# Seven quadrant products in place of eight in twelve gate/up blocks of an FFN, with the weight sums made by accumulating transfers

## The chip, the core and the metric

One core of one Trainium2 chip runs the whole kernel. The metric is the device time of one launch in microseconds. The kernel before took 1153.77 us (median of 3 runs, 1153.56 to 1154.09).

TensorE (PE) multiplies, VectorE (DVE) and ScalarE (ACT) work element by element, GpSimd (POOL) does a few small operations, SyncE (SP) issues the DMA transfers. Each engine works through its own queue in order, and semaphores order the engines among each other.

## The reference

Two layers; each has a first FFN, a mixer (state-space model and chunked attention) and a second FFN. The change is in the two FFNs of each layer.

```python
def rmsnorm(x, g):
    y = xf * lax.rsqrt(jnp.mean(xf * xf, axis=-1, keepdims=True) + RMS_EPS)
    return (y * g.astype(jnp.float32)).astype(x.dtype)

def swiglu(h, w_gate, w_up, w_down):
    return (jax.nn.silu(h @ w_gate) * (h @ w_up)) @ w_down

def reference(x, ...):                    # x: (1, 256, 1024) float32
    for l in range(DEPTH):                # DEPTH = 2
        f1 = swiglu(rmsnorm(x, g[0]), ffn_w_gate[l, 0], ffn_w_up[l, 0], ffn_w_down[l, 0])
        x = x + 0.5 * rmsnorm(f1, g[1])
        m = hybrid_mixer(rmsnorm(x, g[2]), w_in[l], ...)
        x = x + rmsnorm(m, g[3])
        f2 = swiglu(rmsnorm(x, g[4]), ffn_w_gate[l, 1], ffn_w_up[l, 1], ffn_w_down[l, 1])
        x = x + 0.5 * rmsnorm(f2, g[5])
    return x
```

The model width is 1024 and the FFN width 2816.

## The kernel before

The 256 rows of x are two row tiles of 128, t = 0 and t = 1. All weights are packed on the host into 368 chunks of 128 x 1024 float32 (512 KB) in the order of their use. `weight(i)` loads chunk i with one DMA into a `raw` buffer and splits it: ACT copies it to `wh` in a reduced format (fp32r), and DVE writes the rest, `wl = raw - wh`. Activations are split in the same way into `xh` and `xl`. A product of 128 x 128 by 128 x 512 is then three matmuls into one bank of PSUM (`ps`): xh by wh, xh by wl, xl by wh (`mm`, line 400 of the kernel before).

An FFN goes over its width in blocks of 512 (`N_BLK`: five of 512 and one of 256). A block of 512 takes for each row tile a gate product and an up product (`gemm`, four chunks each, six matmuls a chunk and row tile), then the gate's SiLU on ACT, its product with up on DVE, four transposes on PE and the split of their result (`t_split`), and one block later four down chunks (`gemm_wide`: three matmuls for each half of the 1024 columns, so six a chunk and row tile) that add to two `ps` banks for each row tile. So a block has 144 matmuls of 512 columns: 96 for gate and up, 48 for down. The program has 20 blocks of width 512; the change touches 12 of them.

The program is recorded as a graph of operations (`Graph.op`), each with a cost in microseconds, and `schedule` lists them: due times run back from the end (`MARGIN` says how much earlier a stream must be done than its user's due time, `TAU` is the time of six matmuls), and at each step the engine that is free first takes the candidate that is due first. `SLOTS` says how many buffers of a class there are: 4 `raw`, 8 `wh`, 8 `wl`, 28 `blk` of 128 x 512, 8 `ps`. The resulting list sets the order on every engine, and the buffers. The times of the list are plans; on the chip an operation starts when its engine has come to it and its semaphores allow it. A load (`dma`, on SP's queue) waits on DVE's `wl` of the chunk that had its `raw` buffer before. `prep` computes the state-space constants of a layer, mainly in small DVE operations, somewhere in the layer's first FFN. `boundary` ends an FFN or a mixer: norm, residual and the next left-hand sides.

## Time and profile before

| | before |
|---|---|
| runs: median (lowest to highest) | 1153.77 us (1153.56 to 1154.09) |
| span of the profiled execution | 1151.6 us |
| PE busy in the span | 1140.8 us, 99% |
| DVE busy | 788.6 us, 68% |
| ACT busy | 606.3 us, 53% |
| POOL busy | 19.8 us, 2% |
| DMA: moved, mean share of the 16 engines | 205.02 MB, 53.7% on the loads' queue |

The profiled execution is given by its span, from the first to the last instruction; the median of the runs is 2.2 us above it, for what lies outside the first and the last instruction. The rows of the page name engine, line and tiles; a line is mostly that of a helper (`mm` is L400, `act` L358, `tt` L365, the transposes L414), so the tiles tell what is meant: `wh<-raw` is the first half of a conversion, `wl<-raw,wh` the second. "Idle before" tells how long the engine stood just ahead of such an instruction and what ended that. The FFNs take about 8 to 200, 385 to 577, 577 to 770 and 955 to 1145 us of the span, the mixers what is between.

### The profile page before, as it was taken

How to read it: one execution, taken by the hardware profiler on the slowest of the kernel's cores; microseconds unless marked ns; L12 is line 12 of the kernel's file. 1: busy time of each engine (PE TensorE's matmuls, PEld its weight loads, DVE VectorE, ACT ScalarE, POOL GpSimd, SP SyncE). 2: the span in 40 equal slices, each digit the busy share in tenths (PEclk: the TensorE clock that was granted, in tenths of full speed). 3: DMA queues.
4: the chain of work that ended last, by engine and by line, in shares of the span. 5: the costliest groups of instructions: out<-in, count | busy, mean ns of one | idle time of the engine just before them, and what ended most of it. 6: DMA issues, size and time to landing. Idle time of an engine off the chain costs nothing.

```text
span 1151.6 us, 15538 instructions
## 1 busy us (share of the span) xinstructions
PE 1140.8 (99%) x5872; PEld 914.0 (79%) x5872; DVE 788.6 (68%) x1190; ACT 606.3 (53%) x894; POOL 19.8 (2%) x53
## 2 busy tenths in 40 slices
...
GB/s 291 252 195 159 183 219 166 181 164 130 86 189 178 207 200 184 186 182 184 187 220 193 184 150 200 204 177 147 166 110 145 184 198 163 192 192 181 190 165 37
DMA packets 60267, 205.02 MB, mean 178 GB/s; under 512 B 7072, under 2 KB 7840, under 8 KB 60192
## 3 DMA queue, kind: packets, MB, share of 16 engines
q1 hardware_dynamic: 60192, 204.03, 53.7%
...
## 4 chain that ended last, share of the span: by engine, by line
PE 94%; ACT 4%; issue 1%; DMA 0%; SPq 0%; DVE 0%; POOLq 0%; POOL 0%; DVEq 0%
PE ps L400 89%; PE ps L414 4%; ACT utz L358 2%; PE ps L406 1%; ACT blk L358 1%; ACT wh L358 1%; DMA x<-in_x_dram 0%; SPq L341 0%; DVE x L380 0%; POOLq L1139 0%; POOL s L376 0%; DVEq L1139 0%; DVE s L388 0%; POOLq L376 0%
## 5 line engine op out<-in xcount | busy, mean ns | idle before, releaser
L400 PE MATMUL ps<-wh,blk 128*128 128x512 f32 x2944 | 916.4, 400 | 0.0
L400 PEld LDWEIGHTS ps<-wh,blk 128*128 128x128 f32 x2944 | 548.0, 188 | 122.6 <-issue 0.3
L365 DVE TENSOR_TENSOR wl<-raw,wh 128x1024 fp32r<-128x1024 f32 (+1 forms) x370 | 448.7, 1217 | 281.9 <-ACT wh L358 280.6
L358 ACT ACTIVATE wh<-raw 128x1024 fp32r<-128x1024 f32 (+1 forms) x370 | 389.7, 1055 | 374.5 <-PE ps L400 334.1
L400 PE MATMUL ps<-wl,blk 128*128 128x512 f32 x1472 | 551.7, 399 | 0.0
L400 PEld LDWEIGHTS ps<-wl,blk 128*128 128x128 f32 x1472 | 274.8, 188 | 61.1 <-issue 0.3
L358 ACT ACTIVATE blk<-ps 128x512 fp32r<-128x512 f32 (+3 forms) x136 | 78.1, 583 | 121.5 <-PE ps L414 103.3
L365 DVE TENSOR_TENSOR blk<-ps,blk 128x512 fp32r<-128x512 f32 (+2 forms) x104 | 69.0, 666 | 36.1 <-ACT blk L358 34.9
L414 PE MATMUL ps<-ident,blk 128*128 128x128 f32 x432 | 76.8, 273 | 0.2
L414 PEld LDWEIGHTS ps<-ident,blk 128*128 128x128 f32 x432 | 57.0, 140 | 20.1 <-ACT blk L358 1.0
L358 ACT ACTIVATE blk<-ps,s 128x512 f32<-128x512 f32 (+1 forms) x80 | 52.5, 658 | 27.6 <-PE ps L400 25.6
L380 DVE SCALAR_TENSOR_TENSOR blk<-ps,s,blk 128x512 f32<-128x512 f32 (+1 forms) x48 | 33.8, 703 | 15.3 <-PE ps L400 11.5
L376 POOL TENSOR_TENSOR s<-s,mhalf 128x1 f32<-128x1 f32 x24 | 13.8, 574 | 804.0 <-DVE s L388 799.1
L358 ACT ACTIVATE blk<-blk,s 128x128 f32<-128x128 f32 (+1 forms) x64 | 25.8, 444 | 0.0
L400 PEld LDWEIGHTS ps<-utz,bt 128*128 128x128 f32 x128 | 18.1, 191 | 4.0 <-ACT utz L358 2.8
L365 DVE TENSOR_TENSOR blk<-blk,blk 128x512 f32<-128x512 f32 (+3 forms) x38 | 21.1, 577 | 0.1
L358 ACT ACTIVATE utz<-blk 32x128 f32<-32x128 f32 x64 | 20.1, 314 | 1.0
L358 ACT ACTIVATE blk<-blk 64x128 f32<-64x128 f32 (+2 forms) x44 | 17.1, 393 | 6.5 <-DVE blk L380 6.0
L365 DVE TENSOR_TENSOR blk<-blk,e 128x512 f32<-128x512 f32 x32 | 20.3, 677 | 0.0
L400 PE MATMUL ps<-utz,bt 128*128 128x128 f32 x128 | 19.2, 278 | 1.0 <-ACT utz L358 0.8
L365 DVE TENSOR_TENSOR blk<-ps,e 128x512 f32<-128x512 f32 x32 | 19.9, 677 | 0.0
L856 DVE TENSOR_TENSOR_SCAN blk<-mt,blk 128x512 f32<-128x512 f32 x16 | 18.6, 1203 | 0.0
...
## 6 DMA issues: line engine op xcount, KB each, us to landing
raw<-in_wall_dram SPq DMA_DIRECT2D x366, 512.0 KB, 3.5
gain<-in_gains_dram SPq DMA_DIRECT2D x22, 256.0 KB, 4.6
blk<-in_bias_dram SPq DMA_DIRECT2D x8, 256.0 KB, 5.0
raw<-in_wall_dram SPq DMA_DIRECT2D x4, 256.0 KB, 3.5
blk<-in_sp_dram SPq DMA_DIRECT2D x4, 256.0 KB, 4.0
x<-in_x_dram SPq DMA_DIRECT2D x3, 256.0 KB, 5.5
out_dram<-x SPq DMA_DIRECT2D x2, 256.0 KB, 2.0
...
```

What stands on the lines that cost most here:

```text
L358: self.nc.scalar.activation(out=out.ap(), in_=in_.ap(), func=func, **k)
L365: lambda: self.nc.vector.tensor_tensor(out=out.ap(), in0=a.ap(), in1=b.ap(), op=op))
L376: lambda: self.nc.gpsimd.tensor_tensor(out=out.ap(), in0=a.ap(), in1=b.ap(), op=ALU.pow))
L380: return self.g.op("dve", cost, [out], [a, s, b], lambda: self.nc.vector.scalar_tensor_tensor(out=out.ap(), in0=a.ap(), scalar=ap(s), in1= ...
L400: return self.g.op("pe", cost, [out], [lhsT, rhs], lambda: self.nc.tensor.matmul(out.ap(), lhsT=lhsT.ap(), rhs=rhs.ap(), start=start, stop ...
L406: self.nc.tensor.matmul(out.ap(), lhsT=lhsT.ap(), rhs=rhs.ap(), start=start, stop=stop)
L414: lambda o=o, s=s: self.nc.tensor.transpose(o.ap(), s.ap(), self.ident.ap()))
L856: self.g.op("dve", 0.6, [o], [mt, z], lambda o=o, z=z: self.nc.vector.tensor_tensor_scan(out=o.ap(), data0=mt.ap(), data1=z.ap(), initial= ...
```

## The change

In blocks 1 and 3 of each layer's first FFN and blocks 1 to 4 of its second, the gate and up products of both row tiles are taken as one product of 2 by 2 quadrants. The left side has the quadrants a11, a12 (row tile 0, first and second half of the 1024 inputs) and a21, a22 (row tile 1); the right side b11, b21 (gate, two chunks each) and b12, b22 (up). Seven products of sums of quadrants (the Winograd form) give the four results that eight products gave.

- `sums` makes the sums of left quadrants once per FFN: eight DVE additions, four scaled splits (ACT and DVE each) and two negations on ACT.
- `seven` does a block. The weight sums are made in the `raw` buffers: b12, then b21, are negated in place on ACT (four chunks, `raw<-raw`), and `add_to` issues eight accumulating DMAs, 512 KB each, from POOL's queue, with source and destination both in SBUF: b11 += -b12; b12 becomes b22 - b12; b11 += b22; b21 becomes b11 - b21. Between these the contents are converted: 14 conversions for the seven products, where there were 8 for gate and up. The eight `raw` buffers of a block's b quadrants so stay in use for most of the block.
- The products go to the banks p1, p5, p6, p7; ACT copies p1 and DVE reads p5 and p7 in the middle of an accumulation, which then goes on in the same bank. Five DVE additions make the four results from the banks.
- Matmuls of 512 columns in such a block: 84 + 48 in place of 96 + 48. In the whole program 4272 in place of 4416.
- Both row tiles of an FFN are recorded together, block by block (`ffn`).
- `SLOTS`: `raw` 9 for 4, `wh` and `wl` 7 for 8. The planner's costs: a matmul of 512 columns 0.232 for 0.216 us, a scan 1.12 for 0.6; `TAU` 1.395 for 1.355; `MARGIN` of `prep` 40 for 111.6. An accumulating DMA is planned at 0.9 us on POOL and 4.6 us after it.
- `uTz`, two own buffers that were zeroed once, become `blk` buffers that POOL zeroes in each `s5`.

Line numbers grow: `mm` is L416 in the changed kernel, `act` L369, `tt` L376, the transposes L430, `add_to` L380.

```diff
+SEVEN = (((1, 3), (1, 2, 3, 4)), ((1, 3), (1, 2, 3, 4)))
...
-SLOTS = {"blk": 28, "ps": 8, "wh": 8, "wl": 8, "raw": 4, "gain": 2,
+SLOTS = {"blk": 28, "ps": 8, "wh": 7, "wl": 7, "raw": 9, "gain": 2,
          "s1": 16, "s2": 8, "s4": 12, "s16": 8}
-TAU = 1.355
-MARGIN = {"conv": 7.558, "conv0": 3.423, "task": 7.748, "att0": 37.576, "s50": 37.749, "att1": 28.585, "s51": 29.753, "prep": 111.598}
+TAU = 1.395
+MARGIN = {"conv": 7.558, "conv0": 3.423, "task": 7.748, "att0": 37.576, "s50": 37.749, "att1": 28.585, "sums": 8.0, "s51": 29.753, "prep": 40.0}
+ADD_LAT = 4.6
...
+        if a.func == "dma":
+            return ADD_LAT
...
-                b.end = max(b.end, o.end + (DMA_LAT if e == "dma" else HOP))
+                b.end = max(b.end, o.end + (DMA_LAT if e == "dma" else ADD_LAT if o.func == "dma" else HOP))
...
+    def add_to(self, out, in_):
+        return self.g.op("pool", 0.9, [out], [out, in_],
+                         lambda: self.nc.gpsimd.dma_start(out=out.ap(), in_=in_.ap(), accum_op=ALU.add), func="dma")
...
-            cost = n / 2370
+            cost = 0.0049 + n / 2254
...
+    def load(self, i, parts=(slice(0, 1024),)):
+        raw = self.g.buf("raw", [P, 1024])
+        for s in parts:
+            self.last_raw = self.dma(raw[:, s], self.w_d[i][:, s], after=[self.last_raw] if self.last_raw else [])
+        return raw
+
+    def halves(self, raw, parts=(slice(0, 1024),)):
+        wh, wl = self.g.buf("wh", [P, 1024], F32R), self.g.buf("wl", [P, 1024], F32R)
+        for s in parts:
+            self.act(wh[:, s], raw[:, s], AF.Copy)
+            self.tt(wl[:, s], raw[:, s], wh[:, s].bitcast(F32), ALU.subtract)
+        return wh, wl
...
-    def mm_two_k(self, bank, xs, w, first, last):
+    def mm_two_k(self, bank, xs, w, first, last, again=False):
         wh, wl = w
         for i, (xh, _) in enumerate(xs):
             s = slice(i * 512, (i + 1) * 512)
-            self.mm(bank, xh, wh[:, s], first and i == 0, False)
-            self.mm(bank, xh, wl[:, s], False, False)
+            self.mm(bank, xh, wh[:, s], first and i == 0, False, again)
+            self.mm(bank, xh, wl[:, s], False, False, again)
         for i, (_, xl) in enumerate(xs):
-            self.mm(bank, xl, wh[:, i * 512:(i + 1) * 512], False, last and i == len(xs) - 1)
+            self.mm(bank, xl, wh[:, i * 512:(i + 1) * 512], False, last and i == len(xs) - 1, again)
...
+    def wide_step(self, banks, x, w, first):
+        for n in range(2):
+            s = slice(n * 512, (n + 1) * 512)
+            self.mm(banks[n], x[0], w[0][:, s], first, False)
+            self.mm(banks[n], x[0], w[1][:, s], False, False)
+            self.mm(banks[n], x[1], w[0][:, s], False, False)
...
+    def sums(self, xs):
+        self.mode("sums", "bulk")
+        a = []
+        for t in range(2):
+            for hi, lo in xs[t].full:
+                r = self.blk()
+                self.tt(r, hi.bitcast(F32), lo.bitcast(F32), ALU.add)
+                a.append(r)
+        a11, a12, a21, a22 = a
+        self.tt(a22, a21, a22, ALU.add)
+        self.tt(a21, a11, a21, ALU.subtract)
+        self.tt(a11, a22, a11, ALU.subtract)
+        self.tt(a12, a12, a11, ALU.subtract)
+        out = []
+        for r, k in ((a22, -1.0), (a11, 1.0), (a21, 1.0), (a12, 1.0)):
+            hi, lo = self.blk(F32R), self.blk(F32R)
+            self.act(hi, r, AF.Copy, scale=k)
+            self.stt(lo, r, k, hi.bitcast(F32), ALU.mult, ALU.subtract)
+            out.append((hi, lo))
+        hi, lo = self.blk(F32R), self.blk(F32R)
+        for o, v in zip((hi, lo), xs[1].full[1]):
+            self.act(o, v.bitcast(F32), AF.Copy, scale=-1.0)
+        out.append((hi, lo))
+        self.mode()
+        return out
...
+    def seven(self, b, xs, rs, s, acc, pend, first):
+        i = self.chunk[0]
+        assert self.chunk == [i, i]
+        self.chunk = [i + 12, i + 12]
+        t0 = i * 2 * TAU - self.saved
+        self.saved += 2 * TAU
+        for t in range(2):
+            for n in range(12):
+                self.mark[(t, i + n)] = len(self.g.ops)
+
+        def conv(raws):
+            return [self.halves(r) for r in raws]
+
+        self.mode("conv", "main")
+        def minus(raws):
+            for r in raws:
+                self.act(r, r, AF.Copy, scale=-1.0)
+
+        def add(to, raws):
+            for o, r in zip(to, raws):
+                self.add_to(o, r)
+
+        b11 = [self.load(i), self.load(i + 1)]
+        w1 = conv(b11)
+        self.weight(i + 2)
+        b21 = [self.load(i + 3), self.load(i + 4)]
+        w2 = conv(b21)
+        minus(b21)
+        b12 = [self.load(i + 5), self.load(i + 6)]
+        minus(b12)
+        add(b11, b12)
+        w5 = conv(b11)
+        b22 = [self.load(i + 7), self.load(i + 8)]
+        add(b12, b22)
+        add(b11, b22)
+        w6 = conv(b11)
+        self.weight(i + 9)
+        w7 = conv(b12)
+        w3 = conv(b22)
+        self.weight(i + 10)
+        add(b21, b11)
+        w4 = conv(b21)
+        self.weight(i + 11)
+
+        def prod(at, bank, a, w, start):
+            self.mode("main", "main", t0 + at * TAU)
+            pairs = list(zip(self.cols(a[0]), self.cols(a[1])))
+            for u in range(2):
+                self.mm_two_k(bank, pairs[2 * u:2 * u + 2], w[u], start and u == 0, u == 1, not start)
+            self.mode()
+
+        def down(at, c):
+            for t in range(2):
+                self.mode("main", "main", t0 + (at + t) * TAU)
+                self.wide_step(acc[t], pend[t][c], self.weight(i + (2, 9, 10, 11)[c]), first and c == 0)
+            self.mode()
+
+        a11, a12 = xs[0].full
+        s1, s2, s3, s4, a22 = s
+        p1 = self.ps()
+        prod(0, p1, a11, w1, True)
+        k1 = self.blk()
+        self.act(k1, p1, AF.Copy)
+        down(2, 0)
+        prod(4, p1, a12, w2, False)
+        sil = [self.blk(), self.blk()]
+        self.act(sil[0], p1, AF.Silu, scale=rs[0])
+        p5, p6 = self.ps(), self.ps()
+        prod(6, p5, s1, w5, True)
+        prod(8, p6, s2, w6, True)
+        u2, u4 = self.blk(), self.blk()
+        self.tt(u2, p6, k1, ALU.add)
+        self.tt(u4, p5, u2, ALU.add)
+        down(10, 1)
+        p7 = self.ps()
+        prod(12, p7, s3, w7, True)
+        self.tt(u4, p7, u4, ALU.add)
+        prod(14, p5, s4, w3, False)
+        h = [self.blk(), u4]
+        self.tt(h[0], p5, u2, ALU.add)
+        self.stt(h[0], h[0], rs[0], sil[0], ALU.mult, ALU.mult)
+        down(16, 2)
+        prod(18, p7, a22, w4, False)
+        self.tt(u2, p7, u2, ALU.add)
+        self.act(sil[1], u2, AF.Silu, scale=rs[1])
+        self.stt(h[1], h[1], rs[1], sil[1], ALU.mult, ALU.mult)
+        down(20, 3)
+        return [self.t_split(h[t], 4) for t in range(2)]
...
+    def ffn(self, l, f, normed):
         ipost = 1 if f == 0 else 5
         nxt = (l, 2) if f == 0 else (l + 1, 0)
+        xs, rs = (list(z) for z in zip(*normed))
+        acc = [(self.ps(), self.ps()) for _ in range(2)]
+        pend, first, s, pre = None, True, None, [None, None]
         for b, wd in enumerate(N_BLK):
+            if b in SEVEN[l][f]:
+                if s is None:
+                    s = self.sums(xs)
+                pend = self.seven(b, xs, rs, s, acc, pend, first)
+                first = False
+            else:
+                res = []
+                for t in range(2):
+                    sil, h = self.blk(), self.blk()
+                    gb = self.gemm(t, xs[t])
+                    if rs[t] is None:
+                        rs[t] = self.row_scale(t, [self.g.ops[self.mark[(t, 2)]]])
+                    self.act(sil[:, :wd], gb[:, :wd], AF.Silu, scale=rs[t])
+                    up = self.gemm(t, xs[t]) if wd == 512 else gb[:, wd:]
+                    self.stt(h[:, :wd], up, rs[t], sil[:, :wd], ALU.mult, ALU.mult)
+                    res.append(self.t_split(h, wd // P))
+                    if b == len(N_BLK) - 1:
+                        pre[t] = self.pre_gain(t, *nxt)
+                    if pend is not None:
+                        self.gemm_wide(t, acc[t], pend[t], first, False)
+                if pend is not None:
+                    first = False
+                pend = res
             if b == 3:
                 self.gain(l, ipost)
                 if nxt[0] < DEPTH:
                     self.gain(*nxt)
+        out = []
+        for t in range(2):
+            self.gemm_wide(t, acc[t], pend[t], False, True)
+            out.append(self.boundary(t, l, ipost, acc[t], 1.0 / 16, 4.0 * EPS, *nxt, pre[t]))
+        return out
...
-        self.uTz = [self.own(f"utz{i}", [P, 2, 2, 2, 64]) for i in range(2)]
         self.S = [self.own(f"st{i}", [P, PAIRS, 65], F32) for i in range(2)]
-        for t in self.CT + [self.D0] + self.uTz:
+        for t in self.CT + [self.D0]:
...
+        uz = [self.blk() for _ in range(2)]
+        for z in uz:
+            self.memset("pool", z, 0.0)
+        uz = [z.rearrange("p (a b c t) -> p a b c t", a=2, b=2, c=2) for z in uz]
...
-                self.g.op("dve", 0.6, [o], [mt, z], lambda o=o, z=z: self.nc.vector.tensor_tensor_scan(
+                self.g.op("dve", 1.12, [o], [mt, z], lambda o=o, z=z: self.nc.vector.tensor_tensor_scan(
...
-            normed = [self.ffn(t, l, 0, normed[t]) for t in range(2)]
+            normed = self.ffn(l, 0, normed)
...
+        if i in seven:
+            out += [gu[i][:2], dn[i - 1][:1], gu[i][2:], dn[i - 1][1:]]
+        else:
+            out += [gu[i], dn[i - 1]]
```

Three places show the order on the engines. In the names `raw`, `wh`, `wl`, `blk` and `ps` are the buffers above, the number is that of the buffer's content.

PE in the middle of the second FFN of layer 1, before: a chunk of row tile 0's product (`ps_9177`) and then a chunk of row tile 1's (`ps_9168`), three chunks behind; each `wh` with its `wl` comes up once for either row tile.

```order
L400 MATMUL ps_9177<-wh_9123,blk_8632 128x512
L400 MATMUL ps_9177<-wl_9130,blk_8632 128x512
L400 MATMUL ps_9177<-wh_9123,blk_8632 128x512
L400 MATMUL ps_9177<-wl_9130,blk_8632 128x512
L400 MATMUL ps_9177<-wh_9123,blk_8647 128x512 x2
L400 MATMUL ps_9168<-wh_9064,blk_8789 128x512
L400 MATMUL ps_9168<-wl_9071,blk_8789 128x512
L400 MATMUL ps_9168<-wh_9064,blk_8789 128x512
L400 MATMUL ps_9168<-wl_9071,blk_8789 128x512
L400 MATMUL ps_9168<-wh_9064,blk_8801 128x512 x2
```

PE in block 3 of that FFN in the changed kernel: the end of a down chunk (`wh_9984`), then the product of -a22 with the sum in b21 (`wh_9971`, `wh_10015`), which goes on in the bank of p7 (`ps_9994`).

```order
L416 MATMUL ps_9351<-wh_9984,blk_9874 128x512
L416 MATMUL ps_9353<-wh_9984,blk_9874 128x512
L416 MATMUL ps_9351<-wl_9997,blk_9874 128x512
L416 MATMUL ps_9353<-wl_9997,blk_9874 128x512
L416 MATMUL ps_9994<-wh_9971,blk_9244 128x512
L416 MATMUL ps_9994<-wl_9980,blk_9244 128x512
L416 MATMUL ps_9994<-wh_9971,blk_9244 128x512
L416 MATMUL ps_9994<-wl_9980,blk_9244 128x512
L416 MATMUL ps_9994<-wh_9971,blk_9276 128x512 x2
L416 MATMUL ps_9994<-wh_10015,blk_9244 128x512
L416 MATMUL ps_9994<-wl_10024,blk_9244 128x512
L416 MATMUL ps_9994<-wh_10015,blk_9244 128x512
```

A converted chunk of a quadrant product now serves six matmuls in all, where it served twelve, six for each row tile.

ACT at the second FFN of layer 1, before: each `raw` is read once.

```order
L358 ACTIVATE wh_9123<-raw_9062 128x1024
L358 ACTIVATE wh_9141<-raw_9080 128x1024
L358 ACTIVATE wh_9159<-raw_9103 128x1024
L358 ACTIVATE blk_9170<-ps_9101,s_1755_8760 128x512
L358 ACTIVATE wh_9181<-raw_9121 128x1024
L358 ACTIVATE blk_9203<-ps_9194 128x512
L358 ACTIVATE wh_9208<-raw_9139 128x1024
L358 ACTIVATE wh_9224<-raw_9157 128x1024
L358 ACTIVATE wh_9244<-raw_9179 128x1024
```

ACT in block 3 of that FFN, changed; `raw_9673` and `raw_9686` are b11, `raw_9713` and `raw_9725` b21, `raw_9735` and `raw_9749` b12, `raw_9699` is a down chunk.

```order
L369 ACTIVATE raw_9735<-raw_9735 128x1024
L369 ACTIVATE wh_9780<-raw_9699 128x1024
L369 ACTIVATE raw_9749<-raw_9749 128x1024
L369 ACTIVATE wh_9806<-raw_9713 128x1024
L369 ACTIVATE wh_9820<-raw_9725 128x1024
L369 ACTIVATE blk_9829<-ps_9817 128x512
L369 ACTIVATE wh_9834<-raw_9673 128x1024
L369 ACTIVATE blk_9843<-blk_9711,s_2029_9164 128x512
L369 ACTIVATE raw_9713<-raw_9713 128x1024
L369 ACTIVATE raw_9725<-raw_9725 128x1024
L369 ACTIVATE wh_9867<-raw_9686 128x1024
L369 ACTIVATE blk_9874<-ps_9863 128x512
```

Both chunks of b11 are here converted a second time (`wh_9834`, `wh_9867`), which needs the accumulating DMA of the negated b12 into them; behind these rows on ACT stand the other conversions of the block, and the next block's.

POOL, the eight accumulating DMAs of the same block (there was nothing on POOL between the norms of two FFNs before):

```order
L380 DMA raw_9673<-raw_9735 128x1024
L380 DMA raw_9686<-raw_9749 128x1024
L380 DMA raw_9735<-raw_9762 128x1024
L380 DMA raw_9749<-raw_9788 128x1024
L380 DMA raw_9673<-raw_9762 128x1024
L380 DMA raw_9686<-raw_9788 128x1024
L380 DMA raw_9713<-raw_9673 128x1024
L380 DMA raw_9725<-raw_9686 128x1024
```

The DMAs stand in pairs, one for each chunk of a quadrant, and the fifth to eighth read or write what the first four wrote.

SP's loads of such a block come in the order b11, a down chunk, b21, b12, b22, and then the other three down chunks.

## Rows read from the trace of the kernel before

**Rows 1.** The page's first part: busy time, share of the span, instructions.
```profile
PE 1140.8 (99%) x5872; PEld 914.0 (79%) x5872; DVE 788.6 (68%) x1190; ACT 606.3 (53%) x894; POOL 19.8 (2%) x53
```

**Rows 2.** The chain that ended last, its shares by engine.
```profile
PE 94%; ACT 4%; issue 1%; DMA 0%; SPq 0%; DVE 0%; POOLq 0%; POOL 0%; DVEq 0%
```

**Rows 3.** Stretches: each engine's busy us (count), granted clock, DMA share, GB/s.
```profile
core 0: us, PE busy (x) PEld busy (x) DVE busy (x) ACT busy (x) POOL busy (x), PEclk, DMA share, GB/s
0.00:31.00 31.00, 27.65 (x125) 22.16 (x126) 19.98 (x45) 21.81 (x39) 5.33 (x21) 1.00 0.85 299
31.00:64.00 33.00, 33.00 (x148) 26.70 (x147) 31.68 (x110) 16.55 (x20) 0.00 (x0) 1.00 0.72 241
64.00:97.00 33.00, 33.00 (x156) 26.89 (x156) 29.08 (x54) 23.43 (x41) 0.00 (x0) 1.00 0.55 181
...
200.00:390.00 190.00, 189.43 (x1181) 150.52 (x1180) 153.03 (x223) 112.25 (x198) 2.44 (x6) 1.00 0.49 161
...
770.00:955.00 185.00, 184.43 (x1154) 146.15 (x1153) 148.10 (x217) 109.58 (x194) 2.76 (x4) 1.00 0.49 160
955.00:990.00 35.00, 35.00 (x160) 28.39 (x159) 25.25 (x32) 20.55 (x28) 1.65 (x3) 1.00 0.56 184
990.00:1024.00 34.00, 34.00 (x152) 27.50 (x151) 17.06 (x17) 14.73 (x17) 0.00 (x0) 1.00 0.55 184
...
1125.00:1152.00 27.00, 20.34 (x90) 16.13 (x89) 10.13 (x18) 5.54 (x13) 1.10 (x2) 0.94 0.11 39
```

**Rows 4.** Pieces of that chain in order of time, 1000 to 1060 us: start, length.
```profile
1023.13 9.07 PE ps L400 x39
1032.20 0.22 PE ps L414 x2
...
1033.11 23.70 PE ps L400 x102
...
1057.48 2.58 PE ps L400 x11
```

**Rows 5.** Groups of 990 to 1092 us: busy us, mean ns, idle before.
```profile
L365 DVE TENSOR_TENSOR wl<-raw,wh 128x1024 fp32r<-128x1024 f32 x36 | 44.1, 1225 | 45.5 <-ACT wh L358 45.5
L358 ACT ACTIVATE wh<-raw 128x1024 fp32r<-128x1024 f32 x36 | 38.2, 1060 | 50.1 <-PE ps L400 50.1
...
L365 DVE TENSOR_TENSOR blk<-ps,blk 128x512 fp32r<-128x512 f32 x6 | 4.1, 688 | 3.9 <-ACT blk L358 3.9
L358 ACT ACTIVATE blk<-ps,s 128x512 f32<-128x512 f32 x6 | 4.1, 681 | 1.0 <-PE ps L400 1.0
L358 ACT ACTIVATE blk<-ps 128x512 fp32r<-128x512 f32 x6 | 3.6, 599 | 6.7 <-PE ps L414 6.7
```

**Rows 6.** Groups of the whole span.
```profile
L365 DVE TENSOR_TENSOR blk<-blk,blk 128x512 f32<-128x512 f32 (+3 forms) x38 | 21.1, 577 | 0.1
L380 DVE SCALAR_TENSOR_TENSOR blk<-blk,s,blk 128x512 f32<-128x512 f32 x20 | 14.9, 743 | 0.4 <-POOL s L376 0.4
L376 POOL TENSOR_TENSOR s<-s,mhalf 128x1 f32<-128x1 f32 x24 | 13.8, 574 | 804.0 <-DVE s L388 799.1 <-DVE blk L365 4.9
```

**Rows 7.** DMA issues: count, KB each, median us from issue to landing.
```profile
raw<-in_wall_dram SPq DMA_DIRECT2D x366, 512.0 KB, 3.5
...
x<-in_x_dram SPq DMA_DIRECT2D x3, 256.0 KB, 5.5
```

**Rows 8.** A stretch in which loads follow each other, columns as in rows 3.
```profile
10.00:15.00 5.00, 4.97 (x26) 4.09 (x26) 4.66 (x13) 5.00 (x13) 0.00 (x0) 1.00 1.00 401
```

**Rows 9.** Waits: us in total, times, longest; first the engines', then SP's queue.
```profile
ACT wh L358 <- DMA raw<-in_wall_dram: 17.5, 19, 1.8
...
SPq L341 <- DVE wl L365: 820.4, 313, 15.9
```

62 lines of the change are left out of this document (20 added, 42 removed).

## The prediction

> **What bounds the kernel now.** I read the busy times first. PE is busy for 1140.8 us of 1151.6, and DVE has 68%, ACT 53% [rows 1]. The chain that ended last agrees: 94% of it lies on PE [rows 2]. The stretches tell where PE stands still: 3.35 us in the first 31, 0.57 in each mixer, 6.66 in the last 27, and none in the others shown [rows 3]. That holds even from 31 to 64 us, where DVE is busy for 31.68 of 33 us: a nearly full DVE doesn't by itself stop PE. So the kernel is bound by the number of its matmuls, and the price of one is read from the chain: 102 of 512 columns in 23.70 us, 0.2324 us each, and two transposes in 0.22 [rows 4]. (The page's mean for one matmul is longer, because neighbours overlap.) A block takes 144 x 0.2324 + 8 x 0.11 = 34.35 us, which is what lies between the piece at 1023.13 and the one at 1057.48 [rows 4]. The clock column reads 1.00, the 2.4 GHz level, in all stretches but the last [rows 3]; PE stays as dense, so I change nothing for it.
>
> **The change, part by part.**
>
> *Matmuls.* 12 fewer in each of 12 blocks: 144 x 0.2324 = 33.5 us off PE, and all of it on the path as long as PE stays full. The order on PE holds 4272 against 4416 of them. Transposes stay at 8 a block. A changed block has 132 x 0.2324 + 0.88 = 31.56 us of PE, and this is what the other engines have to meet.
>
> *DVE in a changed block.* 18 conversions x 1.225, two splits and five additions with a bank x 0.688 [rows 5], two products x 0.743 [rows 6]: 22.05 + 4.82 + 1.49 = 28.4 us, 90% of 31.56; before, about 17 of 34 [rows 3]. *ACT*: 18 conversions and 4 negations x 1.060, two SiLU x 0.681, three copies out of banks x 0.599 [rows 5]: 23.3 + 1.4 + 1.8 = 26.5 us, 84%. Both fit and cost nothing by themselves; the cover is 3.2 us a block on DVE and 5.1 on ACT. What shrinks is the lead: seven converted chunks for 18 uses in 31.56 us are worth 12 us of PE, where eight for 12 in 34.35 were worth 23.
>
> *Sums of left quadrants.* Per FFN eight additions x 0.577 [rows 6] and four halves x 0.688 on DVE, 7.4 us; six ACT passes x 0.6, 3.6 us. They lie beside the first block. That of layer 1's second FFN shows DVE busy for 25.25 of 35 us [rows 3]; 32.7 still fits. Nothing on the path; uncovered, 4 x 7.4 = 30 us.
>
> *prep* moves from 31 to 97 us to later blocks. There DVE is busy for 60.8 of 66 us [rows 3], some 26 more than two plain blocks need. It leaves the stretch that now needs DVE for block 1 and lies mostly beside plain blocks, which have 17 us of DVE to spare. Nothing. The zeroing of `uTz`'s successors sits on POOL, idle for all but 19.8 us [rows 1]. The planner's new durations change order only, and what better order could win in the mixers is the 1.1 us of rows 3. The longer queue of loads (9 buffers) can touch the 3.35 us at the start; I leave that.
>
> *Bank reads in the middle of a product.* ACT copies p1 behind the first gate product, and the down step (12 matmuls, 2.8 us) lies between that and its continuation; the copy is 0.6 us. Covered; uncovered, 12 x 0.6 = 7 us.
>
> *The accumulating DMAs* are the part that no row shows. From POOL's issue to landing, L: the nearest row is a 512 KB load, 3.5 us [rows 7]. An add has to read its destination too. Loads at full rate move 401 GB/s [rows 8], 1.31 us for 512 KB, so reading twice makes 4.8, and issuing takes something like a POOL operation, 0.574 [rows 6]: L = 5.4 us. The bounds are 3.5, a plain load, and 9.0: the slowest landing of the page, 5.5, plus a whole further load, 3.5 [rows 7]. I take 5.4, nearest to the load of equal size.
>
> What L does is read from the order. ACT negates the first b12 chunk (1.06 us), then that chunk's add; ACT converts the sum, and behind it on ACT's queue stand a SiLU, two negations and the second b11 chunk's conversion, L + 6.0 us from the start; DVE's half brings it to L + 7.2. Then comes the second add to that chunk (2L + 7.2), then the add into b21's second chunk (3L + 7.2). That add frees the buffer for which SP's queue waits with the next block's b21 load; behind it on SP stands the next b12 load, which lands 1.31 + 3.5 us later, and ACT can negate again. A block that follows a changed block so can't take less than **3L + 12.0**. With L = 5.4 this is 28.2 us and PE's 31.56 hides it; at L = 6.5 they are equal, and from there each us of L costs 3 us at each of the 6 places where a changed block follows another (1 to 2, 2 to 3, 3 to 4 in both second FFNs). The plain block between blocks 1 and 3 of the first FFNs gives the chain time.
>
> Some scatter will come through the thinner lead. ACT waited 19 times for a load, 17.5 us in all, 0.92 each [rows 9], without harm to PE. I price one such wait at each of the 6 places: 5.5 us, with 0 and 12 x 0.92 = 11 as bounds.
>
> SP's waits have so far been on DVE, 820.4 us in 313 [rows 9], which is only the pacing of the loads. Now some are on an add, and all loads behind such a one wait too; that is in the loop above. POOL's own powers in the norms stand between the FFNs' adds, not behind any that is late.
>
> The Trainium skill, SBUF — State Buffer, "SBUF: two separate sides", says that a DMA issued by GpSimd can stall because GpSimd can't write its descriptors while VectorE runs in a two-port mode, and that `tensor_tensor` does not enter one. The conversions are `tensor_tensor` [rows 5]; by that page L stays free of DVE's load. No row shows it.
>
> **The sum.** Span 1151.6 - 33.5 + 5.5 = 1123.6 us; the median stood 2.2 above the span, so 1125.8, say **1126 us**.
>
> **The rivals.**
>
> *Late adds (slower).* If L is 9.0, the loop is 39.0 us, 7.4 over PE's 31.56: 6 x 7.4 = 45 us, 1120.3 + 45 = 1165. It is the slower side's mechanism: it costs from L = 6.5 on and decides from L = 8.4, where 6 x (3L + 12.0 - 31.56) has eaten the 33.5. For it: adds come in pairs and beside loads. Against: it needs more than a further half on top of 5.4. Chance 0.10.
>
> *The DMA engines are full.* A block's 12 loads at 1.31 take 15.7 us of them; the 8 adds at twice that 21.0; 36.7 is 5.1 over 31.56, at the 6 places 31 us: 1151. With adds at 1.31 it is 26.2 and nothing. For it: at 184 GB/s the share is already 0.55 [rows 3]. Against: in 10 to 15 us the engines took 401 GB/s [rows 8]. Chance 0.10, of this 0.07 still faster. The Trainium skill, DMA: Bandwidth & Descriptors, "Issuing engines are not separate DMA queues", speaks for it: transfers of all queues share the same 16 engines and interleave. By its fabric ceiling of 435 GB/s the block would need (12 + 16) x 1.2 = 34 us, an estimate, and the sum would be about 1135.
>
> *POOL's issuing holds up DVE.* Eight issues a block at POOL's 0.574 [rows 6] make DVE 33.0 us, 1.4 over, in 12 blocks 17 us: 1137. At a conversion's 1.225 each it is 38.2, 79 us, 1199. For it: DVE has only 3.2 us to give. Against: nothing in the rows; POOL hardly works there, so they settle it neither way. Chance 0.10, of this 0.08 faster.
>
> That PE isn't shortened is out: the order has the 144 matmuls less.
>
> **How the numbers follow.** Forecast 0.70, its own range 1116 to 1134 (no stall and a gain at the start; 11 us and some more of scatter). Low end 1116. The high end reaches to 1150, nearly the full-DMA case and a loop with L up to 8.2; beyond lies most of the late adds, half of the full DMA and the dear end of POOL. Inside: 0.66 of the forecast, 0.05 of the DMA case, 0.08 of the POOL case, some of the late adds, 0.80 in all. Faster by over 0.2% (below 1151.5; about what a measurement of this kernel can tell from no change): 0.70 + 0.07 + 0.08 = 0.85. Within 0.2%: 0.02. Slower: 0.13.
>
> **What would show it.** Right: 4272 matmuls at 0.232 us; pieces of PE near 31.6 us a changed block; PE at 99% of a span near 1124; DVE near 90% in blocks 1 to 4 of the second FFNs; issue to landing of the POOL DMAs below 6.5 us. Late adds: ACT's `wh` waiting for DMA `raw<-raw` and PE for ACT, from block 2 of the second FFNs, while in the first FFNs PE stays full. Full DMA: share 1.00 there, and loads far above 3.5 us. POOL in the way: `wl` above 1.225 us or POOL rows as long as DVE's. Wrong in another way: PE idle at the entry to an FFN (sums) or while prep runs.

## The result, and the profile after

The changed kernel took 1223.65 us (median of 4 runs, 1220.0 to 1228.08), the kernel before, on the same chip, 1153.93 us (4 runs, 1153.56 to 1154.12): 1.0607 times as long, 95% interval 1.0583 to 1.0631. The forecast was 1126 us, faster, with 1150 as the high end. It was wrong, in sign and in size. The profiled execution has a span of 1221.0 us, 97.4 more than the 1123.6 of the sum.

The page after, its busy times and its DMA queues (packets, MB, share of 16 engines' span); [rows 1] are the busy times before.

```profile
PE 1145.6 (94%) x5728; PEld 894.2 (73%) x5728; DVE 925.8 (76%) x1370; ACT 732.1 (60%) x1050; POOL 125.2 (10%) x155
...
q1 hardware_dynamic: 60192, 204.03, 47.8%
q0 software_dynamic: 13824, 50.34, 22.5%
```

PE has 144 instructions fewer and still is busy for 4.8 us more; 75 us of the span it stands still, 11 before. q1 holds the loads, q0 the 96 accumulating transfers. From these rows: 0.225 x 1221.0 / 96 = 2.86 us of all 16 DMA engines for one accumulating transfer of 512 KB, and 0.478 x 1221.0 for 204.03 MB, which is 1.50 us for a load of 512 KB. Both are means over the whole span, also over stretches in which the engines have room; by the same sum a load took 1.59 us in the kernel before (53.7% of 1151.6).

The chain that ended last, shares of the span by engine [rows 2 before], and the issues (KB each, median us from issue to landing) [rows 7 before]:

```profile
PE 50%; DMA 22%; issue 10%; DVE 8%; ACT 7%; POOL 2%; SPq 0%; POOLq 0%; DVEq 0%; ACTq 0%
```

```profile
raw<-in_wall_dram SPq DMA_DIRECT2D x366, 512.0 KB, 4.8
raw<-raw POOLq DMA_DIRECT2D x96, 512.0 KB, 7.7
```

Before, 94% of the chain was PE; now half is, and the transfers `raw<-raw` come next. A load lands in 4.8 us, 3.5 before.

Pieces of the chain in blocks 1 to 3 of the second FFN of layer 1 (start, length, what):

```profile
1023.80 8.54 DMA raw<-raw
...
1032.45 1.07 ACT wh L369
...
1035.07 9.74 DMA raw<-raw
...
1045.34 9.48 DMA raw<-raw
...
1054.90 1.07 ACT wh L369
...
1063.51 8.59 DMA raw<-raw
```

In the first of these blocks three adds stand in a row, with a conversion between, then the next block's first add: the loop that the prediction describes, with L near 9.3 us where it took 5.4. The stretches from one block's first add to the next one's, in the same FFN (columns as in [rows 3]):

```profile
core 0: us, PE busy (x) PEld busy (x) DVE busy (x) ACT busy (x) POOL busy (x), PEclk, DMA share, GB/s
1023.20:1061.60 38.40, 32.44 (x137) 24.07 (x136) 29.14 (x32) 25.47 (x31) 7.00 (x9) 1.00 1.00 259
1061.60:1100.60 39.00, 33.91 (x146) 25.84 (x146) 26.80 (x28) 24.51 (x28) 6.92 (x8) 1.00 1.02 272
1100.60:1140.00 39.40, 34.76 (x142) 26.27 (x141) 26.58 (x27) 24.51 (x28) 6.92 (x8) 0.96 0.99 266
```

A changed block takes 38 to 39 us, not 31.56, and the DMA engines' share is 1.00 at only 260 to 270 GB/s ([rows 8] had 1.00 at 401). In the second FFN of layer 0 the same periods are 39.1, 37.8 and 39.4 us. The queues and issues in these three periods alone, 1023.2 to 1140 us:

```profile
q0 software_dynamic: 3456, 12.58, 59.1%
q1 hardware_dynamic: 5044, 18.39, 41.0%
...
raw<-in_wall_dram SPq DMA_DIRECT2D x36, 512.0 KB, 6.0
raw<-raw POOLq DMA_DIRECT2D x24, 512.0 KB, 7.9
```

Here an add takes 0.591 x 116.8 / 24 = 2.88 us of the engines and a load 0.410 x 116.8 / 36 = 1.33, so the mean of 1.50 is too high for this stretch. The views leave two readings: the loop of waits, 3 x 9 + 12 = 39, or full DMA engines, 12 x 1.33 + 8 x 2.88 = 39.0. The second sum says no more than that the share is 1.00; but its terms are found elsewhere too, 1.31 for a load in [rows 8], 2.90 for an add in e13_half_on_vector below, with a share of 0.80. The two readings give the same number, and each can feed the other, since a full engine makes L long. The experiments have to part them. (Their expectations go by the means over the span, 12 x 1.50 + 8 x 2.86 = 40.9.)

The clock was to stay at 1.00. It doesn't where PE has stood still:

```profile
65.00:70.00 5.00, 2.69 (x11) 1.55 (x9) 2.96 (x3) 2.55 (x3) 0.00 (x0) 1.00 0.99 316
70.00:75.00 5.00, 2.58 (x6) 2.11 (x7) 4.46 (x5) 2.40 (x3) 0.00 (x0) 0.57 0.93 345
75.00:80.00 5.00, 5.00 (x18) 3.94 (x18) 3.30 (x5) 2.87 (x3) 0.00 (x0) 0.75 0.94 345
80.00:85.00 5.00, 5.00 (x23) 4.08 (x22) 4.81 (x7) 3.13 (x4) 0.00 (x0) 1.00 0.81 248
```

PE is busy for 2.69 and 2.58 of 5 us, in the first FFN of layer 0; the granted clock falls to 0.57 in the second of these stretches and is 0.75 in the one after, so part of the time at the 1.2 GHz level, and there PE does 18 matmuls in 5 us instead of 23 once it is back at 1.00. A wait costs more than its own length.

### The profile page after: what moved, and what is told of

Same layout as the page of the kernel before. It is cut to its first block, busy times and chain, and to the rows that moved or that the text cites. A ratio compares the mean times of both kernels' runs of the same rounds, so it can differ in the third digit from the quotient of the medians.

```text
span 1221.0 us, 15977 instructions
## 1 busy us (share of the span) xinstructions
PE 1145.6 (94%) x5728; PEld 894.2 (73%) x5728; DVE 925.8 (76%) x1370; ACT 732.1 (60%) x1050; POOL 125.2 (10%) x155
## 3 DMA queue, kind: packets, MB, share of 16 engines
q1 hardware_dynamic: 60192, 204.03, 47.8%
## 4 chain that ended last, share of the span: by engine, by line
PE 50%; DMA 22%; issue 10%; DVE 8%; ACT 7%; POOL 2%; SPq 0%; POOLq 0%; DVEq 0%; ACTq 0%
PE ps L416 46%; DMA raw<-raw 20%; DVE wl L376 4%; ACT blk L369 4%; ACT wh L369 3%; PE ps L430 3%; DMA raw<-in_wall_dram 2%; DVE blk L376 2%; PE ps L422 1%; POOL s L391 1%; DVE blk L395 1%; POOL raw L380 1%; DVE x L395 1%; SPq L352 0%; ACT L369 0%
## 5 line engine op out<-in xcount | busy, mean ns | idle before, releaser
L416 PE MATMUL ps<-wh,blk 128*128 128x512 f32 x2848 | 897.8, 405 | 44.9 <-ACT wh L369 14.9
L376 DVE TENSOR_TENSOR wl<-raw,wh 128x1024 fp32r<-128x1024 f32 (+1 forms) x442 | 527.0, 1216 | 230.1 <-ACT wh L369 225.8
L416 PEld LDWEIGHTS ps<-wh,blk 128*128 128x128 f32 x2848 | 536.0, 191 | 181.9 <-ACT wh L369 25.3
L369 ACT ACTIVATE wh<-raw 128x1024 fp32r<-128x1024 f32 (+1 forms) x442 | 454.7, 1051 | 353.2 <-PE ps L416 182.1
L416 PE MATMUL ps<-wl,blk 128*128 128x512 f32 x1424 | 530.7, 405 | 5.4 <-DVE wl L376 5.4
L416 PEld LDWEIGHTS ps<-wl,blk 128*128 128x128 f32 x1424 | 271.5, 191 | 72.7 <-DVE wl L376 12.2
L380 POOL DMA_DIRECT2D raw<-raw x96 | 83.6, 920 | 388.6 <-DMA raw<-raw 150.0
L369 ACT ACTIVATE blk<-ps 128x512 fp32r<-128x512 f32 (+3 forms) x148 | 84.2, 579 | 64.4 <-PE ps L430 44.3
L376 DVE TENSOR_TENSOR blk<-ps,blk 128x512 fp32r<-128x512 f32 (+2 forms) x164 | 108.8, 671 | 10.0 <-ACT blk L369 9.6
L430 PE MATMUL ps<-ident,blk 128*128 128x128 f32 x432 | 80.7, 278 | 9.4 <-DVE blk L395 9.4
L430 PEld LDWEIGHTS ps<-ident,blk 128*128 128x128 f32 x432 | 55.3, 141 | 31.9 <-DVE blk L395 16.3
L369 ACT ACTIVATE blk<-ps,s 128x512 f32<-128x512 f32 (+1 forms) x68 | 43.3, 652 | 36.0 <-PE ps L416 33.2
L369 ACT ACTIVATE raw<-raw 128x1024 f32<-128x1024 f32 x48 | 49.8, 1050 | 14.0 <-DMA raw<-in_wall_dram 11.0
L369 ACT ACTIVATE blk<-blk 32x128 f32<-32x128 f32 (+3 forms) x132 | 51.9, 397 | 1.6
L376 DVE TENSOR_TENSOR blk<-blk,blk 128x512 f32<-128x512 f32 (+3 forms) x70 | 42.1, 625 | 2.1 <-ACT blk L369 1.9
L369 ACT ACTIVATE blk<-blk,s 128x128 f32<-128x128 f32 (+2 forms) x76 | 34.6, 485 | 3.0 <-DVE s L1081 2.9
L395 DVE SCALAR_TENSOR_TENSOR blk<-blk,s,blk 128x512 f32<-128x512 f32 x44 | 32.3, 744 | 0.1
L376 DVE TENSOR_TENSOR blk<-ps,e 128x512 f32<-128x512 f32 x32 | 19.8, 680 | 5.0 <-PE ps L416 5.0
L416 PE MATMUL ps<-blk,bt 128*128 128x128 f32 x128 | 19.3, 284 | 3.0 <-ACT blk L369 2.9
L416 PEld LDWEIGHTS ps<-blk,bt 128*128 128x128 f32 x128 | 17.1, 191 | 6.9 <-ACT blk L369 5.1
```

Of the source, the lines that this page charges most:

```text
L369: self.nc.scalar.activation(out=out.ap(), in_=in_.ap(), func=func, **k)
L376: lambda: self.nc.vector.tensor_tensor(out=out.ap(), in0=a.ap(), in1=b.ap(), op=op))
L380: lambda: self.nc.gpsimd.dma_start(out=out.ap(), in_=in_.ap(), accum_op=ALU.add), func="dma")
L395: return self.g.op("dve", cost, [out], [a, s, b], lambda: self.nc.vector.scalar_tensor_tensor(out=out.ap(), in0=a.ap(), scalar=ap(s), in1= ...
L416: return self.g.op("pe", cost, [out], [lhsT, rhs], lambda: self.nc.tensor.matmul(out.ap(), lhsT=lhsT.ap(), rhs=rhs.ap(), start=start, stop ...
L430: lambda o=o, s=s: self.nc.tensor.transpose(o.ap(), s.ap(), self.ident.ap()))
```

## The experiments

Times are single runs beside the kernel before unless an interval is given; the kernel before took 1152.56 to 1155.03 us beside them. The changed kernel's own four runs differ by 8 us, so a few us between two single runs tell nothing.

### Taking the adds away, making them small, making them plain copies

All three keep the plan of the changed kernel, so every engine's order.

```diff
-lambda: self.nc.gpsimd.dma_start(out=out.ap(), in_=in_.ap(), accum_op=ALU.add), func="dma")
+lambda: None, func="dma")                                          # e1_no_adds
+lambda: self.nc.gpsimd.dma_start(out=out[:, 0:32].ap(), in_=in_[:, 0:32].ap(), accum_op=ALU.add), func="dma")   # e2_tiny_adds
+lambda: self.nc.gpsimd.dma_start(out=out.ap(), in_=in_.ap()), func="dma")   # e3_plain_copies
```

> The 96 accumulating DMAs are left out; order, conversions, negations and all products stay as planned (so the weight sums aren't formed). If the loss is the adds' (late or filling the DMA engines), 1126 us as forecast without them, 1118 to 1135, and the distance between the first b12 negations of neighbouring changed blocks falls from 39 to about 31.6 us. If it is the fuller DVE and ACT or the new order, it stays above 1190.

> Each accumulating DMA moves 32 of the 1024 columns, 16 KB in place of 512 KB; number, order and waits stay (the sums are formed for these columns only). If the adds' own transfer time is what counts, issue to landing falls from 7.7 to about 3 us, the loop 3L + 12 to 21 us, under PE's 31.6, and the time to 1118 to 1140. If the fixed cost of issuing on POOL and of the semaphores is what counts, landing stays above 6 us and the time above 1180.

> The same 96 transfers of 512 KB from the same queue, as plain copies without accumulation (so a sum's place holds its second term). If it is reading the destination that makes an add dear (2.86 us of all 16 engines against 1.50 for a load), a copy takes 1.3 to 1.6 us of them, lands in 4 to 5 us, and the time falls to 1120 to 1150. If transfers inside SBUF from POOL's queue are dear whatever they do, 1200 to 1225 as with adds.

Measured: 1133.92 us without adds, 1134.7 with tiny ones, 1146.06 with plain copies. So the adds cost 90 us, and neither their issuing nor their waits at a small L cost any of it: the tiny adds, 2.6 us each to landing, leave periods of 29.4 to 31.5 us in the second FFNs. The page of e1_no_adds, the first line, and the queue and issues of e3_plain_copies:

```profile
PE 1115.9 (99%) x5728; PEld 888.5 (78%) x5728; DVE 922.8 (82%) x1370; ACT 731.3 (65%) x1050; POOL 41.7 (4%) x59
```

```profile
q0 software_dynamic: 13824, 50.34, 11.3%
...
raw<-raw POOLq DMA_DIRECT2D x96, 512.0 KB, 4.6
```

The same bytes without the addition take 0.113 x 1144.3 / 96 = 1.35 us of the engines, less than half of 2.86, and land in 4.6 us instead of 7.7. The addition itself is what is dear. (It also makes the waits longer: with L = 4.6 the loop 3L + 12.0 is 25.8 us, hidden by PE, so the copies don't part the two readings.) The e1 row also says where the 88.9 us of span between it and the changed kernel lie: 29.7 are PE's busy time, for the same 5728 instructions (1145.6 against 1115.9, with the clock's mean at 0.985 against 0.997), and 59.2 are PE standing still.

### All of the change but the changed blocks

```diff
-SEVEN = (((1, 3), (1, 2, 3, 4)), ((1, 3), (1, 2, 3, 4)))
+SEVEN = (((), ()), ((), ()))                                       # e4_no_sevens
```

> The rest of the change alone: no block with seven products, but the new costs, margins, numbers of buffers, the row tiles recorded together and the zeroed blk buffers. If the rest is neutral, 1149 to 1158 us; if the new order or the seven converted chunks cost something of their own (the mixers are 4 us longer each), 1160 to 1175.

Measured: 1161.52 us, ratio 1.007 (1.0053 to 1.0087). The rest of the change costs 8.2 us. From here to e1_no_adds the changed blocks, without their adds, bring 27.6 us, of the 33.5 of the forecast.

### Waits without bytes

```diff
 def add(to, raws):
-    for o, r in zip(to, raws):
-        self.add_to(o, r)
+    for _ in range(3):
+        for o, r in zip(to, raws):
+            self.add_to(o, r)
...
-out=out.ap(), in_=in_.ap(), accum_op=ALU.add
+out=out[:, 0:32].ap(), in_=in_[:, 0:32].ap(), accum_op=ALU.add
...
-ADD_LAT = 4.6
+ADD_LAT = 1.5
...
-return self.g.op("pool", 0.9, [out], [out, in_],
+return self.g.op("pool", 0.3, [out], [out, in_],
```

> Each adding transfer is replaced by three of 32 columns (16 KB) in a row into the same place, each waiting for the one before, so the sums in the weights are left incomplete and the output is not the reference's. A tiny add landed in 2.6 us in e2_tiny_adds, so a link takes about 7.8 us, as the 512 KB add does in the changed kernel (7.7 us), with hardly any DMA time (3 x 2.5% of the span instead of 22.5%). Theory of the latency loop (3L + 12 us between two changed blocks that follow one another): 3 x 7.8 + 12 = 35.4 us or more per block in the second FFNs, so 1155 to 1185 us. Theory of the full DMA engines (12 loads x 1.50 + 8 adds x 2.86 = 40.9 us per block): nothing is left of it, 30 to 31.5 us per block and 1134 to 1140 us, as with one tiny add.

Measured: 1306.87 us. The period in the second FFNs is 41.8 to 50.3 us, at half the DMA share; the first one in layer 0:

```profile
438.18:480.97 42.79, 34.91 (x136) 26.31 (x134) 29.60 (x46) 25.69 (x31) 20.94 (x25) 0.92 0.54 143
```

Both ranges were missed, by far. POOL's queue is in order: the pair that adds b22 to b12 stands between the other three pairs there, so a block has four such chains in a row and not three, each 3 x 2.4 us and POOL's waits. The planner's durations of an add differ too, so the order need not be that of the changed kernel. The run shows that waits alone, with DMA engines that are half idle, can make a loop this slow. It doesn't tell how much of the changed kernel's loss they are.

### Bytes without waits

```diff
-out=out.ap(), in_=in_.ap(), accum_op=ALU.add
+out=self.scr[self.k], in_=in_.ap(), accum_op=ALU.add               # e10_adds_into_scratch
```

> Each adding transfer is issued at the same place from the same source, 512 KB with the addition, but adds into a scratch region of DRAM that nothing reads; so the sums in the weights are left out and the output is not the reference's. Nobody waits for the result, only the source buffer is held until it was read. Theory of the latency loop: the loop is gone, 30 to 32.5 us per block in the second FFNs, 1134 to 1150 us. Theory of the full DMA engines: if these transfers take about as much DMA time as those of the changed kernel (22.5% of the span, 2.86 us of all 16 engines each), 38 to 41 us per block stay and the time is 1190 to 1230 us; if their DMA time is another, 18 us plus 8 times that time gives the block.

```diff
+self.nc.gpsimd.tensor_copy(self.pace.ap(), in_[:, 0:1].ap())       # e12_adds_nobody_waits
-self.nc.gpsimd.dma_start(out=out.ap(), in_=in_.ap(), accum_op=ALU.add)
+self.nc.gpsimd.dma_start(out=self.scr[self.k], in_=self.x[0].ap(), accum_op=ALU.add)
```

> At the place of each addition GpSimd copies one column of the source chunk (so that it waits as before) and issues a 512 KB adding transfer from the fixed residual block x into a scratch region of DRAM. The sums in the weights are left out, the output is not the reference's; no weight buffer waits for such a transfer, on either side, so no loop through the buffers is left, only the transfers' share of the DMA engines. In e10_adds_into_scratch the source chunks were still held until the transfer had landed (13.2 us). Theory of the full DMA engines: 12 x 1.50 + 8 x 2.8 = 40 us per block where changed blocks follow one another, and 1180 to 1215 us in all. Theory that buffers held during the additions make the loop: 30 to 32.5 us per block and 1134 to 1150 us.

Measured: 1199.15 us with the source still held, 1195.9 with no weight buffer tied to the adds at all. The three periods of layer 0 in e12_adds_nobody_waits, and its queue:

```profile
420.73:459.00 38.27, 31.45 (x139) 25.21 (x138) 30.25 (x46) 25.52 (x31) 11.20 (x18) 0.96 0.98 263
459.00:497.37 38.37, 35.73 (x150) 28.45 (x149) 29.94 (x49) 25.49 (x29) 9.35 (x16) 0.95 1.02 284
497.37:535.24 37.87, 33.56 (x141) 26.54 (x140) 26.70 (x27) 24.55 (x28) 9.64 (x17) 0.95 1.01 276
```

```profile
q0 software_dynamic: 13824, 50.34, 22.2%
```

ACT's waits for loads in that run (us in total, times, longest), 17.5, 19 and 1.8 in [rows 9]:

```profile
ACT wh L370 <- DMA raw<-in_wall_dram: 53.8, 33, 7.7
```

No product waits for an add here, no buffer is held by one, and the block still takes 38 us: the loads come too late, because the DMA engines are full. DVE's busy time is 925.4 us, 922.8 without adds, so the issuing on POOL doesn't slow it. That decides for the engines; 62 of the 90 us are there before anyone waits for an add. (These adds write to DRAM, and POOL copies a column ahead of each; the engine time of an add, 2.77 us over the span, is near the 2.86 of the changed kernel.)

### Room for the loop, and half the bytes

```diff
-"blk": 28, ... "raw": 9
+"blk": 24, ... "raw": 11                                           # e11_raw11_blk24
```

> Two more raw buffers (11 for 9), paid for with four fewer blk (24 for 28); the computation is complete. Theory of the latency loop: loads of the next changed block can start two chunks earlier, so the loop loosens by about the time between two buffer releases (some 3 us each, 6 in all): about 33 us per block and 1170 to 1195 us, if the fewer blk cost nothing. Theory of the full DMA engines: 38 to 41 us per block stay, 1215 to 1235 us.

```diff
-out=out.ap(), in_=in_.ap(), accum_op=ALU.add
+out=out[:, 0:512].ap(), in_=in_[:, 0:512].ap(), accum_op=ALU.add   # e20_half_size_adds
```

> The changed kernel with adding transfers of 512 of 1024 columns (256 KB), so the sums in the weights are half done and the output is not the reference's. Theory of the full DMA engines: 12 x 1.50 + 8 x 1.43 = 29.4 us per block where changed blocks follow one another, below TensorE's 31.6, so 31 to 33 us per block and 1138 to 1160 us in all. If waiting for the additions' results is the larger part, a quarter less landing time at most is saved by each, 36 us per block and more remain and the time stays above 1180 us.

Measured: 1212.16 and 1150.4 us. One steady period of each, e11_raw11_blk24 first:

```profile
1089.42:1127.92 38.50, 35.42 (x145) 27.80 (x144) 26.86 (x27) 24.52 (x28) 6.91 (x8) 0.91 1.04 278
```

```profile
477.80:511.04 33.24, 33.15 (x147) 26.39 (x147) 27.66 (x29) 24.43 (x28) 6.89 (x8) 1.00 0.94 257
```

Two more buffers leave the steady period at 38.5 us with the share over 1: they only help at the entry (the first periods are 35.1 and 36.3). The total lies between the two ranges that were expected; the period is that of the full engines. Half the bytes, with the same number of adds and waits, bring PE back to 33.15 of 33.24 us (periods of 31.3 to 35.0), and 73 us of the 90 are gone. Bytes weigh, as full engines would have it. But this run doesn't part the readings by itself: its adds land in 4.9 us, not the quarter less that was expected, and 3 x 4.9 + 12.0 = 26.7 is under PE's time too.

### Adding on another engine

```diff
-self.nc.gpsimd.dma_start(out=out.ap(), in_=in_.ap(), accum_op=ALU.add)
+self.nc.gpsimd.tensor_tensor(out=out.ap(), in0=out.ap(), in1=in_.ap(), op=ALU.add)   # e6_adds_on_gpsimd
...
-def add(to, raws):
+def add(to, raws, dve=False):                                      # e13_half_on_vector
...
-self.add_to(o, r)
+self.tt(o, o, r, ALU.add) if dve else self.add_to(o, r)
...
-add(b12, b22)
-add(b11, b22)
+add(b12, b22, True)
+add(b11, b22, True)
```

> The eight additions of a changed block are done by GpSimd as tensor_tensor on 128x1024 instead of by transfers; the computation is complete, the planner still thinks of transfers. DMA time falls to that of the loads (about 48 to 53% of the span). Theory of the full DMA engines: gains what the transfers cost, unless GpSimd is slow: at 2 us each and 16 us per block, 1140 to 1160 us. Theory of the latency loop: L becomes the GpSimd time of two additions in a row; at 2 us each L is 4 and the loop 24 us, under TensorE's 31.5, also 1140 to 1160 us. If GpSimd's reading of SBUF beside VectorE's two-input instructions slows it as it slowed the power (0.55 to 5.2 us in the changed kernel), additions of 5 us and more make 40 us per block, above 1200 us.

> Four of a changed block's eight additions (b12 plus b22 and b11 plus b22, two chunks each) are done by VectorE as tensor_tensor on 128x1024, four stay adding transfers; the computation is complete. VectorE gets 4 x 1.2 = 4.9 us more per block, 28.4 + 4.9 = 33.3; DMA work falls to 12 x 1.50 + 4 x 2.86 = 29.4 us. Theory of the full DMA engines: about 33.5 us per block, set by VectorE, and 1140 to 1165 us in all. If instead the order on POOL or the planner's wrong times hold the block up, 36 us and more per block remain and the time stays above 1180 us.

Measured: 1279.21 us with all on GpSimd, 1170.86 with half on VectorE; neither beats the kernel before. Two groups of DVE in e6_adds_on_gpsimd from 430 to 475 us, its additions on POOL, and a steady period and the adds' queue of e13_half_on_vector:

```profile
L376 DVE TENSOR_TENSOR wl<-raw,wh 128x1024 fp32r<-128x1024 f32 x18 | 29.4, 1670 | 0.9 <-ACT wh L369 0.9
...
L376 DVE TENSOR_TENSOR blk<-ps,blk 128x512 f32<-128x512 f32 x2 | 1.4, 682 | 0.0
```

```profile
L380 POOL TENSOR_TENSOR raw<-raw,raw 128x1024 f32<-128x1024 f32 x96 | 284.8, 2992 | 243.3 <-DVE wl L376 133.9 <-ACT raw L369 89.4 <-DMA raw<-in_wall_dram 16.3
```

```profile
1027.42:1062.43 35.01, 34.15 (x150) 26.92 (x150) 33.53 (x35) 26.63 (x30) 3.44 (x5) 1.00 0.80 237
```

```profile
q0 software_dynamic: 6912, 25.17, 11.9%
```

An addition on GpSimd takes 2.99 us, and beside it VectorE's conversions take 1.67 us, 1.216 in the changed kernel. So the time above 1200 us came with additions shorter than the 5 us that were expected for it: what they cost is VectorE's time, 1091.4 us busy against 925.8. VectorE's additions with one input in a bank stay at 0.682 us, 0.688 in [rows 5]. The Trainium skill, SBUF — State Buffer, "SBUF: two separate sides", says that GpSimd reading SBUF and a VectorE instruction with two SBUF inputs share one pair of ports, which one of them holds for its whole instruction while the other waits; the traces agree, as the conversions read both inputs from SBUF and these additions only one. With four additions on VectorE (1.22 us each) the DMA share falls to 0.80, each of the 48 adds left still takes 0.119 x 1169.1 / 48 = 2.90 us of the engines, and VectorE is the next bound: 33.53 of 35.01 us. The periods are 31.9 to 36.6 us, and the total is 6 us above the range expected. From these rows one can also estimate that no split gains much: the engines have (31.56 - 12 x 1.33) / 2.88 = 5.4 adds a block to give, VectorE (31.56 - 28.4) / 1.22 = 2.6, together just the 8 that are wanted, with no lead left.

### What the rest of the change costs

None of these seven has a changed block. e14_rest_old_buffers and e15_rest_old_numbers are e4_no_sevens with one thing set back; e16, e17 and e18 are the kernel before with one part of the change; e19 and e21 are e4_no_sevens with all set back but what the list names.

```diff
 e14:  raw 9, wh 7, wl 7               ->  raw 4, wh 8, wl 8
 e15:  TAU, matmul, scan, prep margin  ->  as before
 e16:  uTz zeroed once                 ->  uz, blk zeroed in each mixer
 e17:  prep margin 111.598             ->  40
 e18:  TAU, matmul, scan durations     ->  the new ones
 e19:  the new ffn alone
 e21:  the new ffn and uz; numbers and buffers as before
```

> No changed blocks (as e4_no_sevens, 1161.5 us), and the buffer counts of before (raw 4, wh and wl 8 each for raw 9, wh and wl 7). If the seven converted chunks instead of eight cost the 8 us of the rest of the change, it comes back to 1153 to 1155 us; if the planner's numbers do, it stays at 1160 to 1163 us.

> No changed blocks (as e4_no_sevens, 1161.5 us), with the planner's numbers of before (matmul and scan durations, TAU, the margin of the preparation) and the new buffer counts. If the planner's numbers cost the 8 us, 1153 to 1155 us; if the buffers do, 1160 to 1163 us; if each has its half, 1157 us in both runs.

> The kernel before with one part of the change alone: the mixer's two zero-padded operands (uTz before, uz after) are blk buffers zeroed anew by GpSimd in each mixer, not two buffers zeroed once. e4_no_sevens lost 8.2 us without any changed block, in the mixers of both layers above all, and e15_rest_old_numbers still 4.1 us. If the zeroed blocks cost the 4.1 us, 1157 to 1158 us here; if the new order of writing the FFN does, 1153 to 1154 us.

> The kernel before with one part of the change alone: the margin of the mixer's preparation is 40 us for 111.6 us. If the later preparation costs the 4.1 us that e15_rest_old_numbers got back, 1157 to 1158 us; if the planner's durations do, 1153 to 1154 us.

> The kernel before with one part of the change alone: the planner's matmul time, TAU and the scan's time are the new ones. My prediction said that this changes the order only, at no cost: 1153 to 1154 us. If the planner's durations cost the 4.1 us that e15_rest_old_numbers got back, 1157 to 1158 us.

> No changed blocks, and of the rest of the change only the new way of writing the FFN, in which both row tiles' operations of a block stand together before the next block's (old durations, margins, buffer counts and zeroed operands). If it holds the other half of the 8.2 us, 1157 to 1158 us; if the halves only come about together, 1153 to 1155 us.

> No changed blocks, the planner's numbers and the buffer counts of before; what is left of the change is the new way of writing the FFN and the zeroed blocks together, each of which cost nothing alone (e16, e19). With the new buffer counts it was 1157.4 us (e15). 1153 to 1154.5 us: the new buffer counts hold the other 4 us, seen only once the numbers are the old ones; 1157 to 1158 us: the two parts cost 4 us together.

| | us | ratio to before, 95% |
|---|---|---|
| e14, buffer counts set back | 1161.76 | 1.0075 (1.0058 to 1.0091) |
| e15, numbers set back | 1157.44 | 1.0033 (1.002 to 1.0047) |
| e16, zeroed blocks alone | 1153.4 | 0.9997 (0.9987 to 1.0007) |
| e17, margin alone | 1154.38 | 1.0004 (0.9995 to 1.0013) |
| e18, durations alone | 1157.86 | 1.0036 (1.0023 to 1.0049) |
| e19, way of writing alone | 1153.52 | 1.0 (0.999 to 1.0009) |
| e21, numbers and buffers set back | 1153.65 | 1.0 (0.999 to 1.0009) |

The new durations alone cost 4.1 us, though the matmul's new 0.232 us is what [rows 4] give. The new buffer counts cost 4 us under the old numbers (e15 against e21) and nothing under the new ones (e14 against e4_no_sevens). Alone, margin, zeroed blocks and way of writing cost nothing. The costs don't add up part by part. Where they lie is PE's busy time, with the same 5872 instructions; e18_before_new_durations against [rows 1]:

```profile
PE 1145.4 (99%) x5872; PEld 913.8 (79%) x5872; DVE 784.8 (68%) x1190; ACT 607.1 (52%) x894; POOL 19.3 (2%) x53
```

4.6 us more of PE's busy time, so not a wait that PE's rows show as idle. Which neighbours on PE make the matmuls longer stays open.

## Why the prediction was wrong, step by step

| step | forecast, us | measured, us | by |
|---|---|---|---|
| 144 matmuls fewer | -33.5 | -27.6 | e4_no_sevens to e1_no_adds |
| planner, buffers, way of writing, zeroed blocks, prep | 0 | +8.2 | before to e4_no_sevens |
| the adds, loop and scatter | +5.5 | +89.7 | e1_no_adds to after |
| of it full DMA engines | 0 | 62.0 | e1_no_adds to e12 |
| of it sources held by the adds | 0 | 3.2 | e12 to e10 |
| of it waiting for sums, with what the late loads and the clock add to it | 5.5 | 24.5 | e10 to after |

The measured steps sum to 70.3 us; the two kernels side by side differ by 69.7. (The last three depend on the order in which the causes are put in; with latency put in first the split could be another. The 3.2 us of the held sources is less than the 8 us between runs of the changed kernel, so it isn't shown.)

**The price of an accumulating transfer** is the step that failed. The prediction priced the add's latency, by the nearest rows, at 5.4 us, with 9.0 as the bound. Its engine time stood in the sum at nothing, and only inside a rival, at twice 1.31 = 2.62. Measured: 7.7 us in the median, about 9.3 in the chain, and 2.88 us of the engines in the full stretch. The loop 3L + 12.0 fits the chain shown: with 9.25, the mean of the first three adds in the chain shown, it gives 39.8, and 38.4 to 39.4 were measured. But the full engines give 39.0, so that this number came out doesn't speak for the loop. What was wrong is that L was taken as fixed. It was read from rows in which the engines had room; when 39.0 us of transfers are to go through in 31.56, adds and loads hold each other up: a load lands in 6.0 us in that stretch, 3.5 before, and an add in 7.9, where one of 16 KB lands in 2.6.

**The rivals.** *Full DMA engines* was the right one, with a chance of 0.10. Its sign came, a share of 0.99 to 1.02 with loads far above 3.5 us. It was priced at 1151, too low for these reasons. A block needs 39.0 us of the engines and not 36.7, by the add, 2.88 us and not 2.62 (8 times, 2.1 us); the load's 1.31 was nearly right, with 1.33. It was charged at the 6 places where a changed block follows another; the first FFNs, with none, lost 18.1 and 9.6 us against e1_no_adds, from boundary to boundary. There too the engines were full: a share of 1.03 from 35 to 70 us and of 1.00 from 640 to 676, with PE busy for 27.29 of 35 and 31.43 of 36. And PE's longer busy time, with the clock fallen, wasn't in it; how much of it is the clock stays open. The rows of POOL's power at the boundary after the first FFN of layer 0, after and then e1_no_adds, show the first of these losses, 225.36 against 207.28 us:

```profile
225.36 0.55 POOL L391 TENSOR_TENSOR s<-s,mhalf 128x1 f32<-128x1 f32 x1 [8.87 <-DVE s L403]
```

```profile
207.28 0.55 POOL L391 TENSOR_TENSOR s<-s,mhalf 128x1 f32<-128x1 f32 x1 [8.90 <-DVE s L403]
```

The argument against it, that the engines once took 401 GB/s, was read in a stretch of plain loads; with adds among them they are full at 260 to 270. The Trainium skill, DMA: Bandwidth & Descriptors, "Issuing engines are not separate DMA queues", had spoken for this rival, and the trace agrees: loads on SP's queue and adds on POOL's fill the same engines. The prediction's estimate from that page's ceiling, 34 us a block, was below the measured 38 to 39. It did count an add as two copies, but at 1.2 us each; measured were 1.33 for a load and 2.88 for an add. *Late adds* has its sign in the waits of the changed kernel, and that view alone would have convicted it:

```profile
ACT wh L369 <- DMA raw<-raw: 105.4, 52, 5.0
```

But e12_adds_nobody_waits has no such wait and 62 of the 90 us, and the first FFNs, where this rival has PE full, lost 27.7. What is left for it is in the 24.5 us from e10 to after, not shown apart from the late loads and the clock. *POOL's issuing* is out: an issue takes 0.92 us of POOL, and `wl` is 1.216 us long, no longer than [rows 5] before.

**Matmuls.** PE's busy time fell by 30.3 us from e4_no_sevens (1146.2) to e1_no_adds (1115.9), near the 33.5. Its idle time rose by 2.7 us; that the thinner lead did it wasn't tested.

**DVE, ACT, bank reads.** Right: without adds PE is busy for 99% of the span with DVE at 82%.

**Sums.** DVE had the time for them, as said: without the adds PE stands still for 16 us in the whole span. That they coincide with longer operations on POOL was missed: see the last section.

**"Order only".** Wrong by 8.2 us: an order isn't free because no instruction is added, and the planner with the truer matmul time made a worse one.
